# Layer norms with paired affine operations, and one weight split handed out early, in a two-layer decoder trunk

## The chip, the cores and the metric

The kernel runs on one core of one Trainium2 chip. The metric is the device time of one execution in microseconds; lower is better. The engines are TensorE (PE in the profile; PEld is its weight load), VectorE (DVE), ScalarE (ACT), GpSimd (POOL) and SyncE (SP), whose queue issues the DMAs here.

## The reference

Two layers work on 256 tokens of width 1024, all in float32. Each layer is four sub-blocks, and each sub-block ends in a layer norm of the residual stream:

```
x <- LN(alpha*x + 0.5*SwiGLU_1(x))
x <- LN(alpha*x + Mixer(x))          # layer 0: forgetting attention (fox); layer 1: latent attention (MLA)
x <- LN(alpha*x + 0.5*SwiGLU_2(x))
x <- LN(alpha*x + sigmoid(x Wg + bg) * (p[i] Wp))   # the gate
LN(x) = (x - mean) * rsqrt(var + eps) * g + b
```

The SwiGLU blocks have 2816 hidden units. The MLA keys and values are computed once from the stream that leaves layer 0.

## The kernel before

**Products.** Every float32 product is made of three TensorE products. A weight tile is split into a high part (ScalarE copies it, rounded, L246) and a low part (VectorE subtracts, L247), and a product is high·high + high·low + low·high (`mm3`, L602). The activations are split in the same way: `transposed` (L630) lets TensorE transpose four 128x128 blocks of `x` (L614), then ScalarE writes the high half of `xT` (L623) and VectorE the low half (L627).

**Weights.** `Stream` brings them. Raw weights come by DMA into a ring of three buffers (two units of the weight each). A unit is split into one of ten `hl` slots, or into a buffer lent for the time (`otb`, `qk`, `fs`, `ota`, `gb`). The order of units is that of their first use. A slot is free again when the product that used its unit last has been issued, and the next raw load is issued when both units of a raw buffer are split.

**What sets the order.** The program is written out once, in Python, and each engine runs its instructions in that order. When a split is handed out is decided while the program is written. `pump` (L378), called after each product, hands one out if a slot is free, the raw weight is estimated to have arrived, and the estimated time of VectorE and ScalarE is at most 1600 ns ahead of TensorE's. `busy` (L360) keeps these estimates: for VectorE each call adds a fixed part (80 ns, in the feed-forward blocks 150 ns) and 1.05 ns for each element. `ahead` hands out the high half only, and `later` the low half that is still owed. The fox and MLA mixers follow written lists of steps (`FOX`, `ORDER`), in which "f", "a" and "l" are such calls. So a changed estimate moves splits to other places in the queues of ScalarE, VectorE and SP, and nothing else.

**The norms.** Tokens lie in two tiles, `x[0]` and `x[1]` (x_69 and x_70 in the instruction lists below). `ln` (L707) works on one tile: for each half of 512 columns it adds the new part (L683) and takes statistics (L684), both on VectorE. `ln_apply` (L687) combines them (L692), adds eps (L693), and GpSimd raises the result to the power -0.5 (`rs`, L694). Four VectorE operations apply the norm (L702): for each half a first one, (x - mean) * g, and a second one, * rs + b, which needs `rs`. There are 16 such norms. In 15 the four are written half by half; in the last one (`last`) both first ones stand ahead of the second ones.

**Around the change.** At the end of `ffn` (L1002 to L1012) stand the last output products of token tile 0, `ln(0)`, the same products of tile 1 with the transposes of the new `x[0]` inside (`next_x`), and `ln(1)`. After the second feed-forward block of a layer (`ple=True`) comes the gate, `ple` (L1052): a bias product, eight gate weights for tile 0 with the transposes of `x[1]` ahead of weight 6, `post` (sigmoid L1075, product L1076, statistics) and `ln_apply(0)`, then the same for tile 1, where the transposes of the new `x[0]` stand ahead of weight 6. In layer 0 the next block follows at once: `kv_down(0)` (weight `kd`, 320 columns, from `x[0]`), then `H(0, 0)` and `H(1, 0)`, each with four weight units; `H(1, 0)` first runs all products with the high weight parts, has the transposes of `x[1]` after its third unit, and then the products with the low parts; then `kv_down(1)`. The fourth unit of `H(0, 0)` is split into the buffer `otb`.

The fox mixer begins with products of token tile 0 (`VA(0)`, `VC(0)`, `VB(0)`), with the transposes of `x[1]` inside `VC(0)`.

## Time and profile before

| | |
|---|---|
| median of 3 runs | 1055.34 us (1054.34 to 1055.74) |
| the profiled execution | 1054.48 us, of which its span is 1052.7 us |
| TensorE busy | 1037.3 us, 99% of the span |
| VectorE busy | 895.0 us, 85% |
| ScalarE busy | 592.5 us, 56% |
| GpSimd busy | 59.9 us, 6% |

The times of one profiled execution are used throughout; it is 0.86 us below the median. A row of the timeline has the start in us, the time taken in us, the engine, the line of the kernel, the operation, the tile written and those read, and a count; in brackets stands how long the engine had been idle before it, and what ended that. The gate of layer 0 lies at about 485 to 520 us, the fox mixer at 186 to 305 us.

### The profile page before, as it was taken

What the parts mean: (1) busy time and instruction counts of PE and PEld (TensorE: products, weight loads), DVE (VectorE), ACT (ScalarE), POOL (GpSimd) and SP (SyncE); (2) the same over time, 40 slices, a digit from 0 to 9 for tenths busy, and PEclk for the clock granted to TensorE, in tenths of its full rate; (3) what the DMA queues carried; (4) which work ended last, traced back from release to release, by engine and by line L of the source; (5) the groups of instructions that cost most, each with busy time, mean ns of one, the idle gap of its engine ahead of it and who ended that gap; (6) DMA issues with size and microseconds to landing.
All of it is one profiled execution on the core that took longest, in us unless ns stands there. A gap on an engine that the chain in (4) does not pass through costs nothing.

```text
span 1052.7 us, 17554 instructions
## 1 busy us (share of the span) xinstructions
PE 1037.3 (99%) x7085; PEld 949.7 (90%) x7085; DVE 895.0 (85%) x1312; ACT 592.5 (56%) x901; POOL 59.9 (6%) x88
## 2 busy tenths in 40 slices
PE   9999999999999999999899999999999999999996
PEld 8999898999889999998799898988899889898986
DVE  5788976868898979978979899898887989899877
ACT  6565563667745554663465646546776564646541
POOL 0000000123300000000220000000000000000000
PEclk9999999999999999999999999999999999999999
DMA  7855586444736374673564555742444564554732
GB/s 280 307 186 188 194 287 242 161 144 159 257 126 240 120 249 144 219 301 140 190 234 157 201 195 168 277 154 105 151 155 170 184 213 156 184 213 174 279 121 81
DMA packets 37477, 202.74 MB, mean 193 GB/s; under 512 B 3970, under 2 KB 9874, under 8 KB 16532
## 3 DMA queue, kind: packets, MB, share of 16 engines
q1 hardware_dynamic: 37396, 201.63, 54.0%
q8 instruction: 55, 0.90, 0.3%
q14 instruction: 26, 0.21, 0.1%
HBM read 200.55 MB, written 1.06 MB: 192 GB/s over the span
## 4 chain that ended last, share of the span: by engine, by line
PE 68%; DVE 3%; ACT 1%; issue 1%; POOL 0%; DVEq 0%; ACTq 0%; POOLq 0%
PE h L610 37%; PE y L610 21%; PE tr L610 8%; PE tr L614 2%; DVE hl L247 1%; DVE x L702 0%; PE h L614 0%; DVE x L683 0%; DVE st L684 0%; DVE g L1076 0%; ACT hl L246 0%; POOL rs L694 0%; DVE tr L1715 0%; ACT qk L623 0%; ACT P L1340 0%
## 5 line engine op out<-in xcount | busy, mean ns | idle before, releaser
L610 PE MATMUL h<-xT,hl 128*128 128x256 f32 x3144 | 366.9, 278 | 0.2 <-DVE hl L323 0.2
L610 PEld LDWEIGHTS h<-xT,hl 128*128 128x128 f32 x3144 | 362.8, 189 | 2.0 <-ACT xT L623 0.6
L247 DVE TENSOR_TENSOR hl<-raw,hl 128x1024 fp32r<-128x1024 f32 (+4 forms) x273 | 317.3, 1191 | 38.8 <-ACT hl L246 37.6
L246 ACT ACTIVATE hl<-raw 128x1024 fp32r<-128x1024 f32 (+4 forms) x273 | 270.0, 1027 | 72.0 <-DVE raw L302 41.0
L610 PE MATMUL y<-hl,g 128*128 128x512 f32 x336 | 78.6, 391 | 0.0
L610 PEld LDWEIGHTS y<-hl,g 128*128 128x128 f32 x336 | 62.6, 188 | 12.6
L610 PE MATMUL h<-hl,xT 128*128 128x512 f32 (+2 forms) x312 | 68.0, 371 | 0.0
L610 PEld LDWEIGHTS h<-hl,xT 128*128 128x128 f32 x312 | 54.9, 188 | 9.8
L610 PE MATMUL y<-hl,otb 128*128 128x512 f32 x219 | 58.0, 399 | 0.0
L610 PE MATMUL y<-hl,xT 128*128 128x512 f32 (+3 forms) x282 | 52.7, 334 | 0.0
L623 ACT ACTIVATE xT<-tr 128x512 fp32r<-128x512 f32 x28 | 16.3, 597 | 61.7 <-PE tr L614 61.6
L258 DVE TENSOR_TENSOR hl<-raw,hl 128x1024 fp32r<-128x1024 f32 (+2 forms) x42 | 49.7, 1188 | 1.3 <-ACT hl L254 1.2
L254 ACT ACTIVATE hl<-raw 128x1024 fp32r<-128x1024 f32 (+2 forms) x42 | 43.0, 1028 | 9.7 <-DVE raw L302 9.2
L610 PEld LDWEIGHTS y<-hl,xT 128*128 128x128 f32 x282 | 44.1, 188 | 4.6 <-ACT xT L623 0.4
L610 PEld LDWEIGHTS y<-hl,otb 128*128 128x128 f32 x219 | 39.8, 188 | 8.3 <-DVE otb L627 0.3
L610 PE MATMUL y<-hl,ota 128*128 128x512 f32 x177 | 46.7, 398 | 0.1
L694 POOL TENSOR_TENSOR rs<-ve,mhalf 128x1 f32<-128x1 f32 x16 | 15.1, 944 | 522.2 <-DVE ve L693 522.2
L610 PE MATMUL tr<-xT,hl 128*128 128x256 f32 x360 | 42.8, 278 | 0.0
L610 PEld LDWEIGHTS tr<-xT,hl 128*128 128x128 f32 x360 | 42.1, 188 | 0.3
L610 PEld LDWEIGHTS y<-hl,ota 128*128 128x128 f32 x177 | 32.8, 189 | 7.7 <-DVE hl L247 0.6
L820 ACT ACTIVATE P<-h 128x512 f32<-128x512 f32 x33 | 19.7, 596 | 33.2 <-PE h L610 32.8
L294 DVE TENSOR_TENSOR ts<-raw 128x1024 f32<-128x1024 f32 x29 | 35.4, 1222 | 0.6
(324 smaller groups left out, 1638.5 us busy)
## 6 DMA issues: line engine op xcount, KB each, us to landing
raw<-in_ffn_in_dram SPq DMA_DIRECT2D x85, 1024.0 KB, 4.9
raw<-in_ffn_out_dram SPq DMA_DIRECT2D x44, 1024.0 KB, 5.0
raw<-in_pg_dram SPq DMA_DIRECT2D x8, 1024.0 KB, 4.8
raw<-in_mo_dram SPq DMA_DIRECT2D x8, 1024.0 KB, 4.8
raw<-in_kq_dram SPq DMA_DIRECT2D x8, 640.0 KB, 4.2
gb<-in_ln_g_dram SPq DMA_DIRECT2D x8, 512.0 KB, 6.2
gb<-in_ln_b_dram SPq DMA_DIRECT2D x8, 512.0 KB, 7.6
raw<-in_fk_dram SPq DMA_DIRECT2D x4, 1024.0 KB, 5.0
```

Of the source, the lines that this page charges most:

```text
L246: nc.scalar.activation(hi, src, AF.Copy)
L247: nc.vector.tensor_tensor(lo, src, hi.bitcast(F32), op=ALU.subtract)
L254: nc.scalar.activation(hi, src, AF.Copy)
L258: nc.vector.tensor_tensor(lo, src, hi.bitcast(F32), op=ALU.subtract)
L294: tt(s[:, 0:1024].rearrange("p (a b) -> p a b", b=512), r[:, 0:512][:, None, :].to_broadcast([128, 2, 512]), r[:, 512:1536].rearrange("p ( ...
L610: self.nc.tensor.matmul(out, lhsT, rhs, start=start, stop=stop)
L614: self.nc.tensor.transpose(out, in_, self.ident)
L623: self.nc.scalar.activation(hi, src, AF.Copy)
L694: nc.gpsimd.tensor_tensor(rs, ve, self.mhalf, op=ALU.pow)
L820: nc.scalar.activation(gt, ps, AF.Silu)
```

## The change

Three edits. In `ln_apply` every norm now has the order of the last one: first operation of both halves, then second operation of both halves (in the last norm the second half's last operation stays cut in two pieces). The estimate that `ln_apply` books for VectorE becomes 300 + 4·660 = 2940 elements in place of 1200 + 4·512 = 3248, so 323 ns less for each norm. And a new method of `Stream`, `extra`, hands out one split without a product having asked for it, if a slot is free and the raw weight is estimated to be there; unlike `pump` it doesn't look at how far VectorE and ScalarE are ahead. It is called once in `ffn`, after `ln(0)`, in the two blocks that a gate follows.

```
@@ class Stream
+    def extra(self):
+
+        if self.ready < len(self.order) and self.free() and not self.hold and not self.sums_left(self.order[self.ready]):
+            if self.arrives.get(group_of(self.order[self.ready]), 1e12) <= self.pe_t + 500:
+                self.split()
+
@@ ln_apply
-        self.S.busy(dve=1200 + 4 * 512)
-        if last:
-            todo = [(0, 0, 512), (0, 512, 1024)] + [(1, c0, c1) for c0, c1 in ENDS]
-        else:
-            todo = [(i, 512 * n, 512 * n + 512) for n in range(2) for i in range(2)]
-        for i, c0, c1 in todo:
+        self.S.busy(dve=300 + 4 * 660)
+        ends = ENDS if last else ((0, 512), (512, 1024))
+        for i, c0, c1 in [(0, 0, 512), (0, 512, 1024)] + [(1, c0, c1) for c0, c1 in ends]:
@@ ffn
         self.ln(0, z[0], 1.0, 4 * LN_EPS)
+        if ple:
+            S.extra()
```

The order of TensorE's and of GpSimd's instructions is the same in both kernels. On VectorE and ScalarE the same instructions stand in another order at some places. The line numbers of the changed kernel are higher by 3 to 6.

The first place is VectorE's queue at the start of the fox mixer. Here `hl` rows are the low halves of weight splits, `xT` rows the low halves of the transposed `x[0]`, and the last row shown starts the norm of `x[1]`. Before:

```order
L702 SCALAR_TENSOR_TENSOR x_69<-x_69,rs,gb 128x512
L247 TENSOR_TENSOR hl_1941<-raw,hl_1941 128x1024
L627 TENSOR_TENSOR xT<-tr_1947,xT 128x512
L247 TENSOR_TENSOR hl_1957<-raw,hl_1957 128x1024
L627 TENSOR_TENSOR xT<-tr_1962,xT 128x512
L683 SCALAR_TENSOR_TENSOR x_70<-x_70,y_783 128x512
```

Now:

```order
L705 SCALAR_TENSOR_TENSOR x_69<-x_69,rs,gb 128x512 x2
L253 TENSOR_TENSOR hl_1938<-raw,hl_1938 128x1024
L253 TENSOR_TENSOR hl_1947<-raw,hl_1947 128x1024
L633 TENSOR_TENSOR xT<-tr_1952,xT 128x512
L633 TENSOR_TENSOR xT<-tr_1962,xT 128x512
L253 TENSOR_TENSOR hl_1972<-raw,hl_1972 128x1024
L689 SCALAR_TENSOR_TENSOR x_70<-x_70,y_783 128x512
```

Three splits instead of two stand ahead of the norm of `x[1]`, the second of them ahead of both `xT` rows. From here on nearly every split of the fox mixer stands one place earlier, up to its end, where two splits instead of three stand between the products L1361 and the low halves of `PT`.

The second place is VectorE's queue after the first norm of the second feed-forward block of layer 0, where `extra` is called. Before:

```order
L702 SCALAR_TENSOR_TENSOR x_69<-x_69,rs,gb 128x512
L627 TENSOR_TENSOR xT<-tr_5197,xT 128x512
L247 TENSOR_TENSOR hl_5207<-raw,hl_5207 128x1024
L627 TENSOR_TENSOR xT<-tr_5212,xT 128x512
L683 SCALAR_TENSOR_TENSOR x_70<-x_70,y_3992 128x512
```

Now:

```order
L705 SCALAR_TENSOR_TENSOR x_69<-x_69,rs,gb 128x512 x2
L253 TENSOR_TENSOR hl_5167<-raw,hl_5167 128x1024
L633 TENSOR_TENSOR xT<-tr_5202,xT 128x512
L633 TENSOR_TENSOR xT<-tr_5212,xT 128x512
L253 TENSOR_TENSOR hl_5222<-raw,hl_5222 128x1024
L689 SCALAR_TENSOR_TENSOR x_70<-x_70,y_3992 128x512
```

The split handed out by `extra`, hl_5167 (gate weight 5), stands ahead of the `xT` rows, and the next one, gate weight 6, ahead of the norm of `x[1]`; all later splits up to the next block stand one place earlier. After the norm of `x[1]` there follow now one split of 1024 and two of 640 (`kd`), the two `xT` rows and two splits of 640, where two of 1024, `xT` and three of 640 stood. After the norm of `x[0]` in the gate there follow two splits of 1024, where one of 640 and one of 1024 stood.

The third place is VectorE's queue at the norm of `x[1]` in the gate of layer 0; `g` rows are the product with the sigmoid, `otb` the last weight unit of `H(0, 0)`, the `hl` rows after it the first two of `H(1, 0)`. Before:

```order
L702 SCALAR_TENSOR_TENSOR x_70<-x_70,mv,gb 128x512
L702 SCALAR_TENSOR_TENSOR x_70<-x_70,rs,gb 128x512
L702 SCALAR_TENSOR_TENSOR x_70<-x_70,mv,gb 128x512
L702 SCALAR_TENSOR_TENSOR x_70<-x_70,rs,gb 128x512
L1443 TENSOR_SCALAR ve<-ss 128x1
L247 TENSOR_TENSOR otb<-raw,otb 128x1024
L247 TENSOR_TENSOR hl_5515<-raw,hl_5515 128x1024
L247 TENSOR_TENSOR hl_5524<-raw,hl_5524 128x1024
```

Now:

```order
L253 TENSOR_TENSOR hl_5420<-raw,hl_5420 128x1024
L253 TENSOR_TENSOR otb<-raw,otb 128x1024
L1081 TENSOR_TENSOR g_5438<-g_5438,ota 128x512
L689 SCALAR_TENSOR_TENSOR x_70<-x_70,g_5438 128x512
L690 BN_STATS st_5437<-x_70 128x6
L1081 TENSOR_TENSOR g_5438<-g_5438,ota 128x512
L689 SCALAR_TENSOR_TENSOR x_70<-x_70,g_5438 128x512
L690 BN_STATS st_5437<-x_70 128x6
L698 BN_AGGR mv<-st_5437 128x2
L699 TENSOR_SCALAR ve<-mv 128x1
L705 SCALAR_TENSOR_TENSOR x_70<-x_70,mv,gb 128x512 x2
L705 SCALAR_TENSOR_TENSOR x_70<-x_70,rs,gb 128x512 x2
```

The split into `otb` stood behind the whole norm of `x[1]`; now it stands ahead of the product that begins that norm's sums. Behind the norm follow hl_5512 and hl_5521, the units that were hl_5515 and hl_5524.

In layer 1 the same call moves one split ahead of `xT` in the same way; the gate weights 6 and 7 then stand behind the norm of `x[1]`. In the feed-forward blocks a few splits stand one place earlier; the MLA mixer has the order it had.

## The prediction

> **What bounds the kernel now.** I read the page first, then TensorE's waits, then the timelines of TensorE and VectorE around each wait.

> ```profile
> PE 1037.3 (99%) x7085; PEld 949.7 (90%) x7085; DVE 895.0 (85%) x1312; ACT 592.5 (56%) x901; POOL 59.9 (6%) x88
> ```

> TensorE is busy for 99% of the span and its products do not change. So an earlier VectorE is worth something only where TensorE waits for it, and a later one costs something only where TensorE would begin to wait. The two largest such waits on VectorE, by the view of TensorE's waits (total, times, longest):

> ```profile
> PE h L610 <- DVE otb L247: 3.0, 1, 3.0
> PE tr L614 <- DVE x L702: 0.7, 1, 0.7
> ```

> Both lie in the gate of layer 0 and behind it. TensorE there:

> ```profile
> 505.62 0.60 PE L614 MATMUL tr<-ident,x 128*128 128x128 f32 x4
> 506.93 0.63 PE L614 MATMUL tr<-ident,x 128*128 128x128 f32 x4 [0.71 <-DVE x L702]
> ...
> 517.82 0.40 PE L610 MATMUL h<-otb,xT 128*128 128x512 f32 x1
> 521.20 1.43 PE L610 MATMUL h<-otb,xT 128*128 128x512 f32 x5 [2.99 <-DVE otb L247]
> 522.47 2.91 PE L610 MATMUL h<-hl,xT 128*128 128x512 f32 x12
> 525.22 1.03 PE L614 MATMUL tr<-ident,x 128*128 128x128 f32 x8
> ...
> 528.88 3.39 PE L610 MATMUL h<-hl,xT 128*128 128x320 f32 x22
> ```

> In the first wait four blocks of the new `x[0]` are transposed, and the next four wait for the second half of the norm. In the second, the first product with `otb` (high half) starts at 517.82; the next needs the low half and starts at 521.20 instead of about 0.23 later (the next 12 such products start at 522.47, what follows them at 525.22: 2.75/12): 3.15 us are lost. VectorE in the same stretch:

> ```profile
> 496.13 2.29 DVE L247 TENSOR_TENSOR hl<-raw,hl 128x640 fp32r<-128x640 f32 x3
> 498.85 0.69 DVE L1076 TENSOR_TENSOR g<-g,ota 128x512 f32<-128x512 f32 x1 [0.43 <-ACT g L1075]
> ...
> 506.03 0.75 DVE L702 SCALAR_TENSOR_TENSOR x<-x,rs,gb 128x512 f32<-128x512 f32 x1
> 506.70 1.96 DVE L247 TENSOR_TENSOR hl<-raw,hl 128x640 fp32r<-128x640 f32 x2
> ...
> 512.04 0.68 DVE L1076 TENSOR_TENSOR g<-g,ota 128x512 f32<-128x512 f32 x1
> ...
> 519.93 1.22 DVE L247 TENSOR_TENSOR otb<-raw,otb 128x1024 fp32r<-128x1024 f32 x1
> 521.06 2.35 DVE L247 TENSOR_TENSOR hl<-raw,hl 128x1024 fp32r<-128x1024 f32 x2
> ```

> Between 498.85 and 521 VectorE never idles for long: its queue is one chain, and `otb`'s low half stands behind the whole norm of `x[1]`.

> **The pair order.** A norm written half by half, and the last norm, which has the new order already:

> ```profile
> 478.13 0.74 DVE L702 SCALAR_TENSOR_TENSOR x<-x,mv,gb 128x512 f32<-128x512 f32 x1
> 479.32 0.75 DVE L702 SCALAR_TENSOR_TENSOR x<-x,rs,gb 128x512 f32<-128x512 f32 x1 [0.45 <-POOL rs L694]
> ...
> 480.76 0.75 DVE L702 SCALAR_TENSOR_TENSOR x<-x,rs,gb 128x512 f32<-128x512 f32 x1
> ...
> 1046.31 1.40 DVE L702 SCALAR_TENSOR_TENSOR x<-x,mv,gb 128x512 f32<-128x512 f32 x2
> 1046.54 0.92 POOL L694 TENSOR_TENSOR rs<-ve,mhalf 128x1 f32<-128x1 f32 x1 [8.51 <-DVE ve L693]
> 1047.63 1.54 DVE L702 SCALAR_TENSOR_TENSOR x<-x,rs,gb 128x512 f32<-128x512 f32 x3
> ```

> Before, first to last operation takes 480.76 − 478.13 = 2.63 us, 0.45 of it waiting for `rs`. In the last norm two first operations pass in 1047.63 − 1046.31 = 1.32, or 0.66 each, and the wait is gone. Three steps of 0.66 make 1.98, so a norm ends 0.65 earlier. Its first half, though, is ready 1.32 after the first operation instead of 1.19, so 0.13 later. Over 15 norms that would be 9.75 us on VectorE; nearly all lies under TensorE's cover. The place with the wait for `x` gets it.

> Of the 0.65, 0.45 is that wait; the other 0.2 is that a second operation no longer follows the first one of its own half at once. [...]

> **Gate of layer 0.** This is the sum's main term, followed step by step. VectorE around the norm of `x[1]` at its start:

> ```profile
> 483.60 0.69 DVE L627 TENSOR_TENSOR xT<-tr,xT 128x512 fp32r<-128x512 f32 x1 [2.08 <-ACT xT L623]
> ...
> 486.29 0.68 DVE L683 SCALAR_TENSOR_TENSOR x<-x,y 128x512 f32<-128x512 f32 x1
> ```

> The split of `extra` (1.22) fits into the idle 2.08 ahead of 483.60, so it costs nothing; without that cover it would delay `xT` by up to 1.22. The next split now comes behind both `xT` rows, so the norm of `x[1]` starts about 0.6 later; its own 0.65 makes up for it, and it ends when it does now. Behind it stood 2x1024 and 3x640, now 1024 and 4x640: one 640 (2.29/3 = 0.76) for one 1024 (2.35/2 = 1.18), so VectorE is ready 0.41 sooner, near 498.0. The sigmoid must come sooner too:

> ```profile
> 494.92 1.99 ACT L246 ACTIVATE hl<-raw 128x640 fp32r<-128x640 f32 x3
> 496.93 1.28 ACT L1075 ACT_TABLE_LOAD   x1
> ...
> 514.77 1.04 ACT L246 ACTIVATE otb<-raw 128x1024 fp32r<-128x1024 f32 x1
> ```

> ScalarE has two copies of 640 instead of three between `xT` and this load (1.99/3 = 0.66). The first product with the gate then starts near 498.2 instead of 498.85: 0.65. With the norm's own 0.65 the last operation of `x[0]` ends at 506.78 − 1.30 = 505.48. TensorE could start the second four blocks at 505.62 + 0.43 = 506.05 (eight that follow one another take 1.03, four 0.60), so this wait goes: 506.93 − 506.05 = 0.88.

> Then follow 2x1024 instead of 2x640, the `xT` pair and 2x1024, the second of these now `otb`. In sum two 1024 for two 640, with one 1024 moved ahead: the queue to the norm of `x[1]` is 0.39 longer (2.35 − 1.96), its start 512.04 − 1.30 + 0.39 = 511.1. By then `otb`'s low half is done, while TensorE wants it at 517.82 − 0.88 + 0.23 = 517.2. Its high half, done by 515.81 now, must come some 6 us earlier as well, since its copy now stands ahead of the sigmoid of `x[1]`. ScalarE, busy for 56%, has the room, and the raw weight is there:

> ```profile
> 497.71 0.33 SPq L471 DMA_DIRECT2D raw<-in_ffn_in_dram  x1
> raw<-in_ffn_in_dram SPq DMA_DIRECT2D x7, 1024.0 KB, 6.6
> ```

> This load brings `otb`'s weight; with the median 6.6 us it has landed by 504.3. So the wait of 3.15 goes whole, and 0.88 + 3.15 = **4.03 us**.

> **What is late next.** The norm of `x[1]` now ends 0.94 + 0.65 earlier and has `otb` no longer behind it, so the splits of `H(1, 0)` start near 518.4 instead of 521.06, 2.66 earlier. The rest of that queue, in order, holds the `xT` of `x[1]`:

> ```profile
> 526.78 1.28 DVE L627 TENSOR_TENSOR xT<-tr,xT 128x512 fp32r<-128x512 f32 x2
> ```

> Its first low half moves from 526.78 + 0.69 to about 524.8 (524.5 if the idle 0.28 in front of the third split goes as well). TensorE starts `kv_down(1)` at 528.88 − 4.03 = 524.85 and wants this half two products later, 2 x 3.39/22 = 0.3. So the whole 4.03 just passes, with some 0.4 us to spare. If it does not, the gain is bounded below by the queue's own 2.66.

> **Fox, start.** Three splits instead of two stand ahead of the norm of `x[1]`:

> ```profile
> 185.49 0.59 ACT L623 ACTIVATE xT<-tr 128x512 fp32r<-128x512 f32 x1
> ...
> 187.37 0.68 DVE L683 SCALAR_TENSOR_TENSOR x<-x,y 128x512 f32<-128x512 f32 x1
> ...
> 190.44 0.74 DVE L702 SCALAR_TENSOR_TENSOR x<-x,mv,gb 128x512 f32<-128x512 f32 x1
> ...
> 192.66 0.60 PE L614 MATMUL tr<-ident,x 128*128 128x128 f32 x4
> ```

> The second `xT` starts on ScalarE at about 185.2 (0.3 earlier than now, since no copy stands between the two any more; an estimate). The copy for the third split (1.04, as above) comes behind it and ends at 185.2 + 0.59 + 1.04 = 186.8; VectorE's part then takes 1.13 from start to start (278.39 to 279.52, below), until 187.95. The norm starts there, 0.58 later. Its first half is ready at 190.44 + 0.58 + 1.32 + 0.75 = 193.09; TensorE's transposes start at 192.66 today, and from end to start another 0.15 passes (506.78 to 506.93). That is a new wait of 193.24 − 192.66 = 0.58 us. Bounds: nothing if the queue keeps the old start (its first half is then ready in time), and 1.1 if the second first operation is held up (the GpSimd rival).

> **Fox, end.** Two splits instead of three stand ahead of `PT`'s low half:

> ```profile
> 278.39 1.20 DVE L258 TENSOR_TENSOR hl<-raw,hl 128x1024 fp32r<-128x1024 f32 x1
> 279.52 2.55 DVE L247 TENSOR_TENSOR hl<-raw,hl 128x1024 fp32r<-128x1024 f32 x2
> ...
> 282.03 0.40 PE L610 MATMUL h<-PT,g 128*128 128x512 f32 x1
> 282.85 1.09 PE L610 MATMUL h<-PT,g 128*128 128x512 f32 x5 [0.42 <-DVE PT L627]
> ```

> `PT` comes 1.15 earlier, at 280.95 instead of 282.10. TensorE's second product can follow the first by 0.23 instead of 0.82: gain 0.59. Elsewhere splits stand earlier in the queues, and no wait of TensorE of over 0.7 depends on them. One alone stands later: gate weight 6 of layer 1, now right behind the norm of `x[1]`, which itself ends earlier. I put it at nothing; uncovered it would cost one split, 1.13.

> Sum: −4.03 + 0.58 − 0.59 = −4.04. The profiled execution (1054.48) becomes 1050.44; the median lies 0.86 above, so 1055.34 − 4.04 = **1051.3**.

> **The rivals.** *The next wait takes a part.* The low half of `xT` comes too late for `kv_down(1)`: 2.66 instead of 4.03 is gained, 1055.34 − 2.66 − 0.01 = 1052.7. For it: the margin of 0.4 is less than the errors of a sum of twelve steps. Chance 0.13.

> *GpSimd keeps VectorE off.* While `rs` is computed, the second first operation runs beside GpSimd. If it is held up until `rs` is done, the four start at 0, 1.19, 1.85 and 2.51: a norm saves 0.12 instead of 0.65, and its first half comes 0.53 later still. In the gate VectorE is then ready at 498.0 + 0.53 = 498.5 instead of 498.85, so the wait for `x` shrinks by 0.35 + 0.12 = 0.47; the 3.15 still goes, the fox start costs 0.58 + 0.53 = 1.11 and its end gains 0.59: −3.10, so 1052.2. Against it: in the last norm GpSimd worked for 0.92 in the first 1.15 us of the two operations, and they still took 0.66 each. Chance 0.05. [...]

> *The change doesn't do what it says.* If the stall at 517.82 comes from something else, say `otb`'s high half or its raw weight, the low half cannot be moved ahead, and the rest cancels: 1055.3. Against it: the high half was done before the low half was begun, and TensorE had already used it at 517.82; VectorE was in the norm meanwhile. Chance 0.10.

> *Slower: splits in front of the softmax.* From the start of fox on, each split stands one place earlier, so each of the later 7 head pairs may find a split of 1.13 in front of its softmax step. If the steps are on TensorE's path, that is 7 x 1.13 = 7.9 against the 4.0: 1059.2. It decides when VectorE's idle time ahead of the step is under 1.13. Against it:

> ```profile
> 219.94 1.22 DVE L247 TENSOR_TENSOR hl<-raw,hl 128x1024 fp32r<-128x1024 f32 x1 [1.61 <-ACT hl L246]
> ```

> VectorE idles 1.61 here, enough to absorb the shift, and the shift is one split for the whole mixer, not one for each pair. Chance 0.06.

> **How the numbers follow.** Forecast 0.66. About 0.2%, or 2.1 us, is what a measurement of this kernel can tell from no change: below 1053.2 is faster, above 1057.5 slower. Forecast, the partial gain and the GpSimd case are faster, together 0.84; I give 0.82, as the partial gain without the one at the fox end (1055.34 − 2.66 + 0.58 = 1053.26) just falls inside the bound; same 0.10 + 0.02 = 0.12, slower 0.06. The range: down to 1055.34 − 4.03 − 0.59 = 1050.7 if the fox start costs nothing, less 0.5 for the spread of a median; up to 1053.26 plus 0.4 of the same spread, 1053.7. No change and the slower case are left out, 0.16.

> **What would show it.** Right: TensorE's waits hold neither `otb` nor `x` near 500 to 520; a norm's four operations start 0.66 apart; a new wait of about 0.6 for `x` at 192.7; none for `PT` near 282; `kv_down(1)` starts about 4 us earlier. Wrong: a wait of TensorE for `xT` near 525 (the partial gain); first operations 1.2 apart (GpSimd); a wait for `otb` that stays; or VectorE waits ahead of softmax steps between 200 and 280.

## The result, and the profile after

The changed kernel takes 1049.99 us (median of 6 runs, 1048.65 to 1050.83), the kernel before 1055.16 us in the same comparison. The ratio is 0.9954, with a 95% interval of 0.9941 to 0.9966: 3.6 to 6.2 us less. The forecast was 1051.3; the median lies 1.3 below it, and 0.2 below the lower end of the range (1050.7 − 0.5 = 1050.2). The profiled execution took 1049.60 us, its span is 1047.8 us.

TensorE's waits in the changed kernel, by the same view as before (the one at the program's first product and two of 0.2 left out):

```profile
PE h L616 <- ACT hl L327: 0.7, 1, 0.7
PE h L616 <- ACT p L629: 0.5, 1, 0.5
PE h L616 <- DVE hl L329: 0.4, 1, 0.4
PE tr L620 <- issue: 0.3, 1, 0.3
```

Neither `otb`'s 3.0 nor `x`'s 0.7 is left. The first and third of these rows belong to the first microseconds of the program and differ from execution to execution. TensorE's timeline at the four places of the prediction:

```profile
193.08 0.63 PE L620 MATMUL tr<-ident,x 128*128 128x128 f32 x4 [0.33 <-issue]
...
282.41 1.22 PE L616 MATMUL h<-PT,g 128*128 128x512 f32 x6
...
505.34 1.03 PE L620 MATMUL tr<-ident,x 128*128 128x128 f32 x8
...
516.61 1.55 PE L616 MATMUL h<-otb,xT 128*128 128x512 f32 x6
...
523.95 0.63 PE L616 MATMUL h<-ota,xT 128*128 128x512 f32 x2
524.41 3.91 PE L616 MATMUL h<-hl,xT 128*128 128x320 f32 x25
```

The eight transposes follow one another, and so do the six products with `otb` and those with `PT`; the transposes at 193.08 have the new wait (put down to "issue" here). VectorE in the same kernel:

```profile
190.91 1.40 DVE L705 SCALAR_TENSOR_TENSOR x<-x,mv,gb 128x512 f32<-128x512 f32 x2
192.23 1.41 DVE L705 SCALAR_TENSOR_TENSOR x<-x,rs,gb 128x512 f32<-128x512 f32 x2
...
480.49 1.22 DVE L253 TENSOR_TENSOR hl<-raw,hl 128x1024 fp32r<-128x1024 f32 x1
483.32 0.69 DVE L633 TENSOR_TENSOR xT<-tr,xT 128x512 fp32r<-128x512 f32 x1 [1.61 <-ACT xT L629]
...
502.49 1.40 DVE L705 SCALAR_TENSOR_TENSOR x<-x,mv,gb 128x512 f32<-128x512 f32 x2
503.82 1.40 DVE L705 SCALAR_TENSOR_TENSOR x<-x,rs,gb 128x512 f32<-128x512 f32 x2
...
509.75 1.21 DVE L253 TENSOR_TENSOR otb<-raw,otb 128x1024 fp32r<-128x1024 f32 x1
510.88 0.68 DVE L1081 TENSOR_TENSOR g<-g,ota 128x512 f32<-128x512 f32 x1
...
518.12 2.35 DVE L253 TENSOR_TENSOR hl<-raw,hl 128x1024 fp32r<-128x1024 f32 x2
...
521.86 1.22 DVE L253 TENSOR_TENSOR ota<-raw,ota 128x1024 fp32r<-128x1024 f32 x1
522.99 1.28 DVE L633 TENSOR_TENSOR xT<-tr,xT 128x512 fp32r<-128x512 f32 x2
```

`otb` is now split at 509.75, ahead of the gate's norm of `x[1]`, and two first operations pass in 1.32 or 1.33.

TensorE runs the same products in the same order in both kernels, so the start of the same product can be compared, and a place's worth is how that difference changes across it. This leaves out what differs between executions elsewhere. Besides the places of the table two more show in it: near 429 and near 939 us TensorE loses 0.17 and 0.16.

| TensorE at (us in before) | forecast | measured |
|---|---|---|
| fox start, 187 to 197 | +0.58 | +0.51 |
| fox end, 278 to 287 | −0.59 | −0.70 |
| wait for `x`, 500 to 512 | −0.88 | −0.93 |
| wait for `otb` and what follows, 515 to 533 | −3.15 | −3.26 |
| latent attention, 840 to 850 | not in the sum | −0.18 |
| sum | −4.04 | −4.56 |

### The profile page after: what moved, and what is told of

The parts are those of the page before. It is cut to its first block, busy times and chain, and to the rows that moved or that the text cites. A ratio compares the mean times of both kernels' runs of the same rounds, so it can differ in the third digit from the quotient of the medians.

```text
span 1047.8 us, 17555 instructions
## 1 busy us (share of the span) xinstructions
PE 1035.6 (99%) x7085; PEld 948.6 (91%) x7085; DVE 891.8 (85%) x1312; ACT 592.9 (57%) x901; POOL 58.0 (6%) x88
## 4 chain that ended last, share of the span: by engine, by line
PE 95%; DVE 2%; ACT 1%; issue 1%; DMA 0%; SPq 0%; DVEq 0%; ACTq 0%
PE h L616 53%; PE y L616 29%; PE tr L616 10%; PE tr L620 2%; DVE hl L253 1%; PE h L620 1%; DMA raw<-in_w_dram 0%; PE tr L1375 0%; DVE ts L300 0%; DVE x L705 0%; DVE tr L1720 0%; ACT qk L629 0%; DVE PT L633 0%; DVE ts L306 0%; DVE raw L308 0%
## 5 line engine op out<-in xcount | busy, mean ns | idle before, releaser
L253 DVE TENSOR_TENSOR hl<-raw,hl 128x1024 fp32r<-128x1024 f32 (+5 forms) x271 | 314.2, 1190 | 36.1 <-ACT hl L252 35.0
L252 ACT ACTIVATE hl<-raw 128x1024 fp32r<-128x1024 f32 (+5 forms) x271 | 267.8, 1027 | 70.6 <-DVE raw L308 41.3
L264 DVE TENSOR_TENSOR hl<-raw,hl 128x1024 fp32r<-128x1024 f32 (+2 forms) x44 | 52.3, 1192 | 0.8 <-ACT hl L260 0.7
L260 ACT ACTIVATE hl<-raw 128x1024 fp32r<-128x1024 f32 (+2 forms) x44 | 45.2, 1029 | 9.7 <-DVE raw L308 9.1
## 6 DMA issues: line engine op xcount, KB each, us to landing
raw<-in_ffn_in_dram SPq DMA_DIRECT2D x85, 1024.0 KB, 5.0
raw<-in_ffn_out_dram SPq DMA_DIRECT2D x44, 1024.0 KB, 5.0
raw<-in_pg_dram SPq DMA_DIRECT2D x8, 1024.0 KB, 4.9
raw<-in_mo_dram SPq DMA_DIRECT2D x8, 1024.0 KB, 4.8
raw<-in_fk_dram SPq DMA_DIRECT2D x4, 1024.0 KB, 5.6
```

Source lines behind the costliest of these rows:

```text
L252: nc.scalar.activation(hi, src, AF.Copy)
L253: nc.vector.tensor_tensor(lo, src, hi.bitcast(F32), op=ALU.subtract)
L260: nc.scalar.activation(hi, src, AF.Copy)
L264: nc.vector.tensor_tensor(lo, src, hi.bitcast(F32), op=ALU.subtract)
```

## The experiments

Twelve kernels ran in three comparisons, each with runs of the kernel before on the same chip (medians 1055.47, 1056.03 and 1055.86). "Places" below are those of the table, in its order.

**1. The parts, alone and in pairs.** The changed kernel was put back to the old code in one or two of its three parts: the order in `ln_apply`, the number in `busy`, the call of `extra`.

The pair order alone:

```
-        self.S.busy(dve=300 + 4 * 660)
+        self.S.busy(dve=1200 + 4 * 512)
...
-        if ple:
-            S.extra()
```

> The pair order alone, with the old estimate and without the extra split; VectorE's queue is otherwise that of before. Theory (each wait of TensorE ends with the VectorE chain named for it): the wait for x near 507 shrinks by one norm, 0.65; the low half of otb comes two norms earlier, so TensorE's product near 521 starts 1.30 earlier and the wait for otb stays (about 2.3); nothing at the fox start or end; about 0.15 in the latent attention: 1.4 less, about 1053.8. Rival (the shorter norms are what the change lives from): about 4 to 5 less, 1050 to 1051.

Measured 1054.48 us, ratio 0.9988 (0.9980 to 0.9997): 0.3 to 2.1 less. The places: 0.00, −0.02, −0.67, −0.65 up to the product behind the wait, −0.19. As expected, `otb`'s wait shrinks by two norms and stays:

```profile
521.05 2.01 PE L616 MATMUL h<-otb,xT 128*128 128x512 f32 x5 [2.36 <-DVE otb L253]
522.86 3.97 PE L616 MATMUL h<-hl,xT 128*128 128x512 f32 x12
```

One thing was not expected: the 12 products behind it take 3.97 us, where the same products took 2.91 before. Experiment 4 is about this.

The new estimate alone (old order, no `extra`):

```
-        ends = ENDS if last else ((0, 512), (512, 1024))
-        for i, c0, c1 in [(0, 0, 512), (0, 512, 1024)] + [(1, c0, c1) for c0, c1 in ends]:
+        if last:
+            todo = [(0, 0, 512), (0, 512, 1024)] + [(1, c0, c1) for c0, c1 in ENDS]
+        else:
+            todo = [(i, 512 * n, 512 * n + 512) for n in range(2) for i in range(2)]
+        for i, c0, c1 in todo:
...
-        if ple:
-            S.extra()
```

> The new estimate alone, with the norms half by half and no extra split; VectorE's queue has the splits where the changed kernel has them in layer 0. Theory: the wait for x shrinks by only 0.2, the wait for otb (3.15) goes, what is late next (low halves in H(1, 0) and xT of x[1]) comes 2.0 later than in the changed kernel and just about in time (0.2 lost at most); fox start +0.45, fox end -0.6: 3.3 less, about 1051.9. Rival (only norm time matters): 0.5 less at most, 1054.7. Rival (the next chain is already as late as the wait that goes): 2 less, 1053.2.

Measured 1050.48 us, ratio 0.9949 (0.9937 to 0.9961), 4.1 to 6.6 less, which is more than the 3.3. The places, however, are +0.39, −0.70, −0.41, −2.41, −0.19, in sum −3.32. The sum is as expected, but with luck, since two of its parts are not: the wait for `x` shrank by 0.41 instead of 0.2, and at `otb` 2.41 is gained, where at least 2.95 was expected. And the time fell by more than the sum: again experiment 4. Both rivals fall: norm time alone would leave `otb`'s wait, and it is gone; and the sum is 3.3, not 2. What is late next shows in TensorE's timeline:

```profile
505.37 0.63 PE L620 MATMUL tr<-ident,x 128*128 128x128 f32 x4 [0.32 <-DVE x L708]
...
524.33 0.73 PE L616 MATMUL h<-ota,xT 128*128 128x512 f32 x2 [0.59 <-DVE ota L253]
```

It is the low half of `ota`, the fourth weight of `H(1, 0)`, which stands just ahead of `xT` in VectorE's queue, and not `xT`, as the prediction had it.

The pair order and the estimate, without `extra`:

```
-        if ple:
-            S.extra()
```

> The changed kernel without the extra split. Theory: in layer 0 VectorE's queue is then word for word that of the changed kernel, so all steps near 193, 282, 507 and 521 are the same, 1050.0 within 0.5. Rival, as the prediction had it (the extra split in front of xT makes room for the rest): a split stands later in the gate, otb's low half is late again by part of the 3.15, 1052 to 1053.

Measured 1049.80 us, ratio 0.9942 (0.9930 to 0.9954). The places: +0.51, −0.72, −0.93, −3.26, −0.19, the changed kernel's to 0.02. With the new estimate `pump` hands out the same splits at the same places in layer 0, so `extra` changes nothing there; it moves one split in layer 1, and no wait with it. The prediction's sentence that the split of `extra` fits into idle time describes the right queue, but the estimate alone makes that queue.

The pair order and `extra`, with the old estimate:

```
-        self.S.busy(dve=300 + 4 * 660)
+        self.S.busy(dve=1200 + 4 * 512)
```

> The pair order with the extra split, with the old estimate. Theory: the extra split moves one weight past one xT operation and nothing behind it, so this is the pair order alone: 1.4 less, about 1053.8, with the wait for otb near 2.3. Rival (the extra split brings otb ahead of the norm): about 4 less, 1051.

Measured 1053.86 us, ratio 0.9981 (0.9971 to 0.9990). The places: 0.00, −0.01, −0.67, −0.61, −0.19, as for the pair order alone. The wait for `otb` is as long, but here the products behind it ran at their usual pace:

```profile
521.10 1.44 PE L616 MATMUL h<-otb,xT 128*128 128x512 f32 x5 [2.36 <-DVE otb L253]
522.37 2.92 PE L616 MATMUL h<-hl,xT 128*128 128x512 f32 x12
```

**2. The wait for `otb`, and what is late next.** In the kernel before, one split more is handed out ahead of the gate's norm of `x[1]`:

```
                 gate(1, k, full)
+            if li == 0:
+                S.split()
             for c0, c1 in full:
```

> The kernel before with one edit: the split into otb is handed out ahead of the gate's norm of x[1] in layer 0. All norms stay half by half, all else stays. Theory: the wait of 3.15 goes, but the norm of x[1] now ends one split (1.14) later, so the next low halves of H(1, 0) keep their old time, and the low half of ota is late by about 0.9: 2.2 less (2.0 to 2.5), about 1053.0, with a new wait near 525. Rival (nothing is late next): 3.15 less, 1052.0. Rival (the stall comes from something other than the place in VectorE's queue): 0, 1055.2.

Measured 1052.41 us, ratio 0.9963 (0.9951 to 0.9975). At the place TensorE gains 2.01, at all others under 0.05. So the place in the queue is the cause of the 3.15, and about 1.1 comes back a few us later, as the theory said:

```profile
518.39 1.55 PE L610 MATMUL h<-otb,xT 128*128 128x512 f32 x6
519.78 1.08 PE L610 MATMUL h<-hl,xT 128*128 128x512 f32 x4
521.36 2.14 PE L610 MATMUL h<-hl,xT 128*128 128x512 f32 x8 [0.51 <-ACT hl L246]
...
526.88 0.73 PE L610 MATMUL h<-ota,xT 128*128 128x512 f32 x2 [0.19 <-DVE ota L247]
```

Of the two waits the larger is not for the low half of `ota`, though, but for the high half of a split on ScalarE, which in this kernel stood behind an operation (the table load and `P`, L780) that waited 2.29 us for TensorE. The time fell by 2.6 to 5.2 us, again more than the waits.

The other side of it: the changed kernel with needless VectorE work behind that norm.

```
             self.ln_apply(1, st[1][0][:, 0:2, :], LN_EPS)
+            if li == 0:
+                for _ in range(4):
+                    nc.vector.tensor_tensor(st[1][1][:, 0:512], st[1][1][:, 512:1024], self.pj[:, 0, :], op=ALU.mult)
```

> The changed kernel with four needless products of 128x512 on VectorE (about 2.8 us) behind the gate's norm of x[1] in layer 0, ahead of the splits of H(1, 0). Theory: in the changed kernel the low halves of ota and of xT are there 0.7 to 0.9 us ahead of TensorE, so 2.8 costs 1.9 to 2.1: 1052.0, with a wait near 524. Rival (the queue has already no room: every us costs a us): 2.8 more, 1052.8. Rival (far more room than read from the two rows): under 1 more.

Measured 1053.14 us, ratio 0.9968 (0.9956 to 0.9980). TensorE's waits are 0.28, 0.59 and 0.94:

```profile
521.67 1.20 PE L616 MATMUL h<-ota,xT 128*128 128x512 f32 x4 [0.28 <-ACT ota L252]
522.71 1.08 PE L616 MATMUL h<-hl,xT 128*128 128x512 f32 x4
524.37 0.73 PE L616 MATMUL h<-hl,xT 128*128 128x512 f32 x2 [0.59 <-DVE hl L253]
526.05 1.04 PE L616 MATMUL h<-ota,xT 128*128 128x512 f32 x2 [0.94 <-DVE ota L253]
526.88 7.72 PE L616 MATMUL h<-hl,xT 128*128 128x320 f32 x36
```

Idle time counts from the end of a product, which is modelled, so the starts are the better measure: the product at 526.05 starts at 523.95 in the changed kernel, and this execution was 0.40 ahead of it before the place, so it comes 2.50 later. The four operations take 2.78 from start to start. So the room was about 0.3, less than read from the two rows, and the result lies between the theory (1.9 to 2.1) and its first rival (2.8), nearer to the rival. Part of the reason stands in VectorE's and GpSimd's timelines:

```profile
523.29 1.62 POOL L1468 TENSOR_TENSOR PT<-PT,nrm 128x256 f32<-128x256 f32 x1
524.24 1.75 DVE L253 TENSOR_TENSOR ota<-raw,ota 128x1024 fp32r<-128x1024 f32 x1
```

The split into `ota` took 1.22 in the changed kernel and takes 1.75 here, 0.53 more; with it the room comes to 2.78 + 0.53 − 2.50 = 0.81, as the rows had it. The wait of 0.28 for ScalarE is the experiment's own: the added products read the buffer into which `ota` is split, and ScalarE's copy into it waited 1.42 for them.

`kv_down(1)` behind it (36 of its products in 7.72, where the same 36 took 6.44 in the changed kernel, 0.21 a product against 0.18) is slowed again at its start, as in experiment 4. Here too the weights are late first, and no product waits for `xT`.

**3. Cover, and the fox start.** Without the second affine operations of nine norms:

```
+        if n in (0, 2, 3, 8, 9, 10, 11, 12, 13):
+            todo = todo[0:2]
```

> The changed kernel without the second affine operations of 9 of the 16 norms (it leaves out the scaling by rs and the addition of b there): all but the four of the second feed-forward block and gate of layer 0, the one of x[1] at the fox start, and the last two. VectorE does 9 x 1.32 = 11.9 us less. Theory (these norms lie under TensorE's cover, so 0.65 saved in each of them brought nothing): at most 0.4 less, 1049.6 to 1050.0. Rival (VectorE's time counts at large): several us less, in proportion to 11.9.

Measured 1050.22 us, ratio 0.9941 (0.9928 to 0.9954), the changed kernel's to within the interval; between 110 us and the end TensorE's schedule differs from the changed kernel's by 0.3. So 11.9 us less on VectorE bring nothing there, and the prediction's statement that the 0.65 of most norms lies under TensorE's cover is shown for these nine.

The transposes of `x[1]` at the fox start two steps later:

```
-        VC(0, {4: lambda: self.XT(1, (0,)), 7: lambda: self.XT(1, (1,))})
+        VC(0, {6: lambda: self.XT(1, (0,)), 7: lambda: self.XT(1, (1,))})
```

> The changed kernel with one edit: in the first block of fox the transposes of the first half of x[1] stand two steps (0.79 us of products) later in TensorE's order. Theory: the new wait of 0.57 near 193 is only the order, so it goes, and nothing else moves: 0.57 less, 1049.4. Rival (the second half of x[1], or its xT, is then late instead): 0 to 0.3 less, 1049.7 to 1050.0.

In the trace the new wait is gone, and across 191 to 197 TensorE gains 0.50 on the changed kernel:

```profile
193.85 0.60 PE L620 MATMUL tr<-ident,x 128*128 128x128 f32 x4
194.20 0.63 PE L616 MATMUL y<-hl,xT 128*128 128x272 f32 x3
194.66 0.60 PE L620 MATMUL tr<-ident,x 128*128 128x128 f32 x4
```

The time was 1050.96 us, ratio 0.9946 (0.9933 to 0.9958); 0.5 us is less than these intervals can tell. By its trace it is the better version, by its time it isn't shown to be.

**4. What a long wait costs beside its length.** The kernels that remove `otb`'s wait gained more time than their places: the estimate alone 5.0 against 3.3 (difference of medians), the pair order with the estimate 5.7 against 4.6, the split ahead 3.6 against 2.0. Those that keep it did not: 1.0 and 1.6 against 1.5. The traces with slow products (0.43 apart instead of 0.23) had them behind waits. So in the changed kernel one wait of chosen length was put in, at the transposes of `x[0]` in the gate, by 2, 5 or 10 needless operations ahead of the norm's last one:

```
+        def stall():
+            for _ in range(2):
+                nc.vector.tensor_tensor(st[0][1][:, 0:512], st[0][1][:, 512:1024], self.pj[:, 0, :], op=ALU.mult)
...
+            if mid and (i, c0) == (1, 512):
+                mid()
```

> The changed kernel with two needless VectorE products of 128x512 (0.715 each) ahead of the last operation of the gate's norm of x[0] in layer 0, so that TensorE waits once, near 507, for 2 x 0.715 - 0.39 = 1.04. Both theories: 1.0 more than the changed kernel, about 1051.0, with the mean granted clock of the executions as there, 0.9978.

> The same with five such products: one wait of 5 x 0.715 - 0.39 = 3.19, as long as the one that the change removed. Theory (a long wait also lowers TensorE's granted clock behind it in part of the executions, and that costs 1.4 to 1.7 each time, as in the traces of the pair order alone and of the delay): 3.2 and on the mean about 0.9 more, 1054.0, mean clock about 0.9967. Rival (a wait costs its length): 3.2 more, 1053.2, mean clock 0.9976.

> The same with ten such products: one wait of 10 x 0.715 - 0.39 = 6.76. Theory: now every execution has the lower clock behind the wait, 6.8 + 1.5 or more: 1058.3, mean clock 0.996, and products near 515 some 0.43 apart instead of 0.23. Rival (a wait costs its length): 1056.8, mean clock 0.997.

| kernel | wait at the place | TensorE later there than in the changed kernel | median us | mean granted clock |
|---|---|---|---|---|
| 2 operations | 0.76 | 0.95 | 1051.35 (5 runs) | 0.9978 |
| 5 operations | 2.93 | 4.7 | 1054.87 (11) | 0.9968 |
| 10 operations | 6.57 | 9.1 | 1059.30 (11) | 0.9949 |

The ratios to before are 0.9956 (0.9943 to 0.9969), 0.9986 (0.9977 to 0.9995) and 1.0030 (1.0019 to 1.0041). From the first to the second the waits alone are worth 2.2 us, and the medians differ by 3.5; from the first to the third 5.8 and 8.0. TensorE's timeline with the shortest wait:

```profile
507.39 0.63 PE L620 MATMUL tr<-ident,x 128*128 128x128 f32 x4 [0.76 <-DVE x L707]
507.77 3.00 PE L616 MATMUL y<-hl,xT 128*128 128x512 f32 x12
```

with the middle one:

```profile
509.44 0.87 PE L620 MATMUL tr<-ident,x 128*128 128x128 f32 x4 [2.93 <-DVE x L707]
509.96 4.44 PE L616 MATMUL y<-hl,xT 128*128 128x512 f32 x12
```

and with the longest:

```profile
511.78 1.09 PE L620 MATMUL tr<-ident,x 128*128 128x128 f32 x4 [6.57 <-DVE x L707]
512.52 4.97 PE L616 MATMUL y<-hl,xT 128*128 128x512 f32 x12
```

The same twelve products take 3.00, 4.44 and 4.97 us. The view by stretches (busy time, count, granted clock, DMA share, GB/s) names the cause, in the kernel with the middle wait:

```profile
506.28:509.69 3.41, 0.48 (x6) 1.00 0.05 19
509.69:513.10 3.41, 3.41 (x12) 0.50 0.22 34
513.10:516.51 3.41, 3.41 (x22) 1.00 0.89 305
```

The granted clock is 0.50 for 3.41 us behind the wait and 1.00 before and after. Half the clock for 3.41 us is 1.7 us of products, and of the 4.7 that TensorE is later there, 3.1 are reached at the product that waited and 1.6 come behind it. It remained to see whether the kernel before does this too; its first profiled execution didn't (2.91 for the twelve products).

> The kernel before, unchanged, for another profiled execution. Theory: its executions fall into some with a mean clock of 0.998 near 1054.6 and some with 0.994 to 0.996 near 1056.1; if the profiled one is of the second kind, products behind the wait for otb near 521 are 0.43 apart for 2 to 4 us. Rival: products behind the wait are 0.23 apart in both kinds, and what lowers the clock lies elsewhere.

The kernel before again, 1056.43 us (11 runs), ratio 1.0002 (0.9993 to 1.0011):

```profile
522.62 2.22 PE L610 MATMUL h<-otb,xT 128*128 128x512 f32 x5 [2.99 <-DVE otb L247]
524.64 3.73 PE L610 MATMUL h<-hl,xT 128*128 128x512 f32 x12
```

The same wait of 2.99, and this time the products behind it are 0.43 apart, 1.6 us lost in about 3.7. Its stretches, and below them two of the first profiled execution:

```profile
519.57:522.98 3.41, 0.42 (x3) 1.00 0.00 0
522.98:526.39 3.41, 3.41 (x10) 0.50 0.84 274
```

```profile
516.29:519.70 3.41, 1.92 (x9) 1.00 0.00 0
519.70:523.11 3.41, 1.91 (x8) 1.00 0.29 65
```

So the rival (the clock falls elsewhere) is out for this execution. These bounds are not free: in every trace the granted clock changes only at times that lie whole multiples of 3.41 us apart, and the stretches are cut there. That shows what the two executions differ in. Here the whole wait lies in one stretch, and in the next the clock is 0.50; in the first execution the same wait lies half in one and half in the next (1.49 and 1.50 us idle), and the clock stays. The last section has this for the other traces.

The 61 runs of the kernel before in the three comparisons bear out the price: the 14 with a mean clock of 0.998 took 1054.6 us on the mean, the 41 with 0.996 or less 1056.2, a difference of 1.6. The other six had 0.997, which can be either kind, since the mean also counts the program's end, where the clock is 0.50 for 3.1 to 6.6 us with no product left. The changed kernel's six had 0.997 or 0.998.

Executions differ in one more way, which no edit here explains. In 8 of the 14 traces, the kernel before again among them, TensorE falls back by about 1.2 us over some 30 us of the first feed-forward block (between 27 and 61 or between 74 and 108 us), without idle time and with a granted clock of 1.00. The cause stays open. It lies outside all places of the table, but a difference of medians of a few runs can hold a part of it.

## Why the prediction was right, and what it left out

**The bound, and where VectorE counts.** Right. TensorE's order is unchanged, the schedule moved at the named waits and by less than 0.2 at three other places, and 11.9 us taken from VectorE at nine covered norms moved nothing.

**The pair order.** Right: 1.32 for two first operations, so 192.23 + 0.66 − 190.91 = 1.98 from the first start to the last, 0.65 less a norm. Alone it is worth 1.5 at the places, 0.67 and 0.65 of it at the two waits of the gate.

**The GpSimd rival** is refuted by the changed kernel itself. GpSimd computed `rs` while both first operations passed in 503.82 − 502.49 = 1.33:

```profile
502.72 0.92 POOL L700 TENSOR_TENSOR rs<-ve,mhalf 128x1 f32<-128x1 f32 x1 [11.96 <-DVE ve L699]
```

Beside this operation of 128x1, then, VectorE was not held up. Beside a larger one it may have been: in experiment 2 GpSimd's product of 128x256 (L1468) took 1.62, where it took 0.74 in the changed kernel, and the split into `ota` that overlaps it took 1.75 instead of 1.22. That the one slowed the other is a guess; no run separates them. And a norm gains more than the 0.45 of the wait for `rs`: its operations of 0.74 now follow one another by 0.66, while in the kernel before the second one of the second half started 0.77 after the first one of its own half (479.99 to 480.76).

**Gate of layer 0.** Right in mechanism and size: 0.93 and 3.26 for 0.88 and 3.15. The attribution was off in one point: the split moved ahead is the work of the new estimate, and `extra` adds nothing.

**What is late next.** The conclusion held (the whole wait passes), but the step named the wrong tile and mis-sized the room. What is due first is the low half of `ota`, done at 521.86 + 1.22 = 523.08 and wanted at 523.95, so 0.87 less 0.15 from VectorE's end to TensorE's start (506.78 to 506.93 in the kernel before); the first half of `xT` has 524.72 − 523.68 = 1.04 less the same. The forecast was 0.4 for `xT`, and it did not look at the weights ahead of `xT` in the same queue; that these had room too was luck. Nor are these 0.7 to 0.9 safe: when the queue was delayed (experiment 2), about 0.3 was left of them, since the split into `ota` itself took longer there.

**Fox start and end.** Right: +0.51 and −0.70 for +0.58 and −0.59.

**The slower rival** (splits in front of the softmax) did not come: from 200 to 275 TensorE's schedule shifts by no more than 0.35.

**What the sum left out** is the 1.2 us between 4.0 and the measured 5.2. Of it 0.5 are the places themselves: 0.18 is the latent attention, which the prediction put at nothing, and the rest are small errors of each term. The larger part is that the step "a wait costs its length" failed: behind the 3 us wait of the kernel before, TensorE ran at half the clock in one of the two profiled executions, and by their mean clock (0.996 or less) in 41 of 61 runs; it cost about 1.6 us each time, or 1.1 on the mean (mean of all 61 runs less the mean of the 14 at 0.998, 1055.78 − 1054.63). The one profiled execution of the kernel before was of the other kind, so no row of it could show this. In the prediction it is hidden in the 0.86 between that execution and the median, which was carried over whole to the changed kernel; there the median lies 0.39 above the profiled execution (1049.99 − 1049.60). With it the sum is 4.6 + 1.1 = 5.7, against 3.6 to 6.2 measured. The two profiled executions, both without the lower clock, differ by 4.88, near the 4.6 of the places.

## What to carry to other kernels

When a wait goes, price the next item in each queue behind it, in queue order: here the weights ahead of `xT` were due before `xT`. Where a planner sets the order, ask of each edit whether the planner would already do it: one changed estimate moved nearly all the splits that moved, and the call written for the purpose moved none that mattered. And read a long wait of TensorE as its length and the products behind it: compare their spacing with the same products elsewhere, and look at the granted clock there, in more than one execution.

## What the runs showed of the hardware

In each of the 14 traces the changes of TensorE's granted clock lie whole multiples of 3.41 us apart (with 5 operations at 4.52, 509.69, 513.10 and 1049.00 us), and between them it is 1.00 or 0.50. These are the stretches of 3.41 us into which the waits fell, with TensorE's idle time in each:

| trace | wait | idle in the stretches | clock in the next |
|---|---|---|---|
| 2 operations | 0.76 | 0.76 | 1.00 |
| the pair order with `extra` | 2.36 | 1.15 and 1.20 | 1.00 |
| the kernel before | 2.99 | 1.49 and 1.50 | 1.00 |
| needless work behind the norm (three waits) | 0.28, 0.59, 0.94 | 0.28 and 1.53 | 0.50, after the second |
| the pair order alone | 2.36 | 2.36 | 0.50 |
| 5 operations | 2.93 | 2.93 | 0.50 |
| the kernel before again | 2.99 | 2.99 | 0.50 |
| 10 operations | 6.57 | 1.32, 3.41 and 1.84 | 1.00 after the first, 0.50 after the second and third |
